# Fourier products over all 128 rows, with channel 128 and token 128 added as columns on VectorE

## The chip, the cores and the metric

The kernel runs on 1 core of one Trainium2 chip. The metric is the device time in microseconds of one execution. Three runs of the kernel before took 1964.46, 1966.94 and 1972.05 us (median 1966.94). A further execution was profiled; all rows below come from it.

## The reference, cut to what matters

Two layers of a diffusion backbone work on 256 context tokens and 256 latent tokens of width 1024. Each layer projects the normed input with `w_in`, runs three branches (mLSTM, differential attention, a Fourier mixing), merges them under sigmoid gates, projects with `w_out`, and applies a SwiGLU feed-forward. The last layer computes only the latent tokens. The Fourier branch takes the 2-D transform over the tokens and over the 256 channels of each of four groups, and keeps the real part:

```python
def _fourier(u):
    B, T, _ = u.shape
    z = u.astype(jnp.float32).reshape(B, T, FN_GROUPS, FN_GC)
    y = jnp.fft.fftn(z, axes=(1, 3), norm='ortho').real
    return y.reshape(B, T, FN_W).astype(u.dtype)

y = gm * (ym @ w_br_ml) + gd * (yd @ w_br_da) + gf * (yf @ w_br_fn)
```

## The kernel before, in words

**The main stream.** Nearly all work is a list of jobs (`prog`). A job loads 512 KB of weights (`Job.load`, L204) into one of four raw buffers, ScalarE rounds them to fp32r (`wh`, L214), VectorE takes the rest (`wl`, L224), and TensorE multiplies wh by the high part of the activations, wh by the low part, and wl by the high part (L309 to L311 in `proj_t`, L330 to L332 in `proj_n`). SP issues loads up to seven jobs ahead, splits go three jobs ahead. A job of `proj_t` has 24 products, of 512 columns in layer 0 (both segments) and 256 in layer 1 (the latent one alone).

**Side work.** A `side` is a generator that is advanced by `tick`, after each quarter of a job, at a given rate (steps divided by four times the jobs); `drain` runs what is left. The framework's planner sets the order of the instructions on each engine but SP, whose order is that of the program.

**The Fourier branch.** With the symmetry of cosine and sine, a 256-point transform splits into an even part with 129 entries and an odd part with 127. `fold_h` folds the tokens (0 to 128 and 1 to 127), `FoldZ` folds the channels of the weights, and `proj_z` computes the folded z of the four groups early in the layer. 129 does not fit in 128 rows: channel 128 of all groups comes out in rows of their own, `rn` (`last`, L837). z and rn are written to DRAM (`zscr`, `nscr`) and read back by `fourier` (L857 to L866), at job 6 of `gates(0)`.

`fourier` then runs as side `fn` beside the eight jobs of `branch(0)` (main products at L309 to L311; VectorE's L1429 evacuates each job). `ns` is the number of segments: 2 in layer 0, 1 in layer 1. Per group g of four, in fp32:

- burst 1 (`pe`): the transform over channels, even part: a full product (L890) and one with the 4 rows of rn (L891), each per segment; ScalarE copies it out (L892).
- burst 2 (`po`): the odd part (L896), and token 128 as a product with `ns` output rows (`po_x`, L899 and L900); two copies (L901, L902).
- burst 3 (`pu`): the transform over tokens: a product with the `ns` rows of token 128 (L911) and a full one (L913), once for 128 columns and once for 32 columns into `px`, and the odd part (L916); ScalarE copies `pu` out (L922), and in layer 0 VectorE subtracts for the low part (L924).

Burst 3 of a group follows the first bursts of the next one. After the last group `px` is copied out (L927, L929). `proj_fn` in `branch(2)` multiplies the result with the folded `w_br_fn` (L946 and L947 fold, L960 to L981 multiply). Side tiles of PSUM rotate over four buffers; most tiles of SBUF are 32 units of 4 KB per partition.

Of the kernel before, what the change touches and what calls it, by code (L numbers as in the profile page):

```python
# [8 lines left out]
F32 = mybir.dt.float32  # L9
# [18 lines left out]
C_ID, C_SEL, C_RC, C_RS, C_FN, C_END = 0, 128, 130, 386, 642, 1542  # L28
T_COS, T_SIN, T_C, T_S, T_ALT, T_ALT2, T_END = 0, 129, 256, 385, 513, 642, 900
VROW = {"norm1": 0, "norm2": 8, "mlhg": 16, "dahg": 24}  # L30


# [11 lines left out]
def tile_trunk(ctx: ExitStack, tc: tile.TileContext, x, c, cx, c_ctx, w_ada, b_ada, norm_g, w_in, ml_gate_b,  # L44
# [24 lines left out]
    def tmp(n=512, dt=F32):  # L69
        return tpool.tile([128, n], dt, tag="t2", name=nm("t"))  # L70
# [10 lines left out]

    cst = cpool.tile([128, C_FN], F32, tag="cst", name="cst")
    ident = cst[:, C_ID:C_ID + 128]
    sel = cst[:, C_SEL:C_SEL + 2]
    ropec = cst[:, C_RC:C_RC + 256]
    ropes = cst[:, C_RS:C_RS + 256]

# [291 lines left out]
    class AdaPart:  # L379
# [24 lines left out]
        def finish(self, scale, shift):  # L404
            pt = side_ps()
            for b in range(4):
                T.matmul(pt[:, b * 2:b * 2 + 2], lhsT=self.rows[:, b * 128:b * 128 + 128], rhs=sel, start=True, stop=True)
# [386 lines left out]
    def proj_z(l, W, ns, hf, st):  # L794

        nu, nv, w = 129 * ns, 127 * ns, 256 * ns
        per = 1024 // w
        zt = []

        def mk(g, odd):  # L800
            def run(job):
                ps = main_ps()
                if not odd and g % per == 0:
                    zt.append(unit().rearrange("p a n -> p (a n)"))

# [12 lines left out]
                if odd:  # L818
                    S.copy(o[:, nu:], ps[:, n - nv:n])
                else:  # L820
                    S.copy(o[:, :nu], ps[:, :nu])
                yield
                if odd and g == 3:
                    last()
            job = FoldZ(W[:, CZ + 256 * g + 128 * odd:CZ + 256 * g + 128 * odd + 128], KB, 128, run, ns == 2)
            job.odd, job.g, job.wn = odd, g, lambda: st["wn"]
            prog.append(job)

        def last():

            ps = side_ps()
            for k in range(KB):
                for i in range(ns):
                    T.matmul(ps[32 * (k % 4):32 * (k % 4) + 32, :nu], lhsT=st["wn"][:, k, :],
                             rhs=hf[i][k][:, :nu].bitcast(F32), start=(k < 4 and i == 0), stop=(k >= 4 and i == ns - 1))
            rn = tmp()
            S.copy(rn[:, :nu], ps[:, :nu])  # L837
# [3 lines left out]
            st["nscr"] = dpool.tile([128, 258], F32, tag="nscr", name=nm("ns"))  # L841
            nc.sync.dma_start(st["nscr"][:, :nu], rn[:, :nu])
            del zt[:]
            hf.clear()

        for g in range(4):
            mk(g, False)
            mk(g, True)
            prog[-1].mate, prog[-2].mate = prog[-2], prog[-1]

    def fourier(l, ns, st):
# [9 lines left out]
        rn = tmp()  # L861
        for g in range(4):
            nc.sync.dma_start(rn[32 * g:32 * g + 4, :nu], st["nscr"][g:128:32, :nu])
        w128 = unit().rearrange("p a n -> p (a n)")
        G.memset(w128, 0.0)
        nc.sync.dma_start(w128[31:128:32, :], w_br_fn[l, 128:1024:256, :])  # L866
        st["w128"] = [w128]
        yield
        if ns == 2:
            wh, wl = (unit(FR).rearrange("p a n -> p (a n)") for _ in range(2))  # L870
# [1 line left out]
            G.tensor_tensor(out=wl, in0=w128, in1=wh.bitcast(F32), op=ALU.subtract)  # L872
            st["w128"] = [wh, wl]
        yield
        px = side_ps()
        res = {}
        cur = None
        for g in range(5):
            prev, cur = cur, None
            if g < 4:  # L880

                z = zt[g // per][:, g % per * w:g % per * w + w]
                row = slice(32 * g, 32 * g + 4)
                ct = unit()
                xt = tmp(129)
                cur = g, ct, xt
                pe = side_ps()
                for s in range(ns):
                    c, o = slice(129 * s, 129 * s + 128), slice(129 * s, 129 * s + 129)
                    T.matmul(pe[:, o], lhsT=z[:, c], rhs=tab[:, T_C:T_C + 129], start=True, stop=False)  # L890
                    T.matmul(pe[:, o], lhsT=rn[row, c], rhs=tab[row, T_ALT:T_ALT + 129], start=False, stop=True)  # L891
                S.copy(ct[:, 0, :nu], pe[:, :nu])  # L892
                yield
                po = side_ps()
                for s in range(ns):
                    T.matmul(po[0:127, 128 * s:128 * s + 128], lhsT=z[:, nu + 127 * s:nu + 127 * s + 127],  # L896
                             rhs=tab[:, T_S:T_S + 128], start=True, stop=True)
                po_x = po[32 * g:32 * g + ns, 256:385]
                T.matmul(po_x, lhsT=z[:, 128:nu:129], rhs=tab[:, T_C:T_C + 129], start=True, stop=False)  # L899
                T.matmul(po_x, lhsT=rn[row, 128:nu:129], rhs=tab[row, T_ALT:T_ALT + 129], start=False, stop=True)  # L900
                S.copy(ct[0:127, 1, :128 * ns], po[0:127, :128 * ns])  # L901
                S.copy(xt[32 * g:32 * g + ns, :], po_x)  # L902
                yield
            if prev is not None:
                q, ct, xt = prev
                row = slice(32 * q, 32 * q + ns)

                pu = side_ps()
                for o, i in ((pu[:, :nu], 0), (px[32 * q:32 * q + 32, :nu], 97)):
                    n = 128 if i == 0 else 32  # L910
                    T.matmul(o, lhsT=xt[row, i:i + n], rhs=tab[row, T_ALT2:T_ALT2 + nu], start=True, stop=False)  # L911
                    for s in range(ns):
                        T.matmul(o[:, 129 * s:129 * s + 129], lhsT=ct[:, 0, 129 * s + i:129 * s + i + n],  # L913
                                 rhs=tab[:, T_COS:T_COS + 129], start=False, stop=(s == ns - 1))
                for s in range(ns):
                    T.matmul(pu[:, nu + 127 * s:nu + 127 * s + 127], lhsT=ct[0:127, 1, 128 * s:128 * s + 128],  # L916
                             rhs=tab[0:127, T_SIN:T_SIN + 127], start=True, stop=True)
# [13 lines left out]
        yield

# [398 lines left out]
    def plan(l, xget, fin, bd1, bd2, bdn):  # L1331
# [278 lines left out]
def make_consts():  # L1610
# [53 lines left out]
```

## Time and profile before

| what | value |
| --- | --- |
| median of three runs | 1966.94 us (1964.46 to 1972.05) |
| the profiled execution | 1967.22 us, span 1965.5 us |
| TensorE busy | 1910.6 us, 97% of the span |
| VectorE, ScalarE, POOL busy | 1193.9, 782.6 and 142.6 us |
| the chain that ended last | TensorE 79%, VectorE 10%, DMA 4%, ScalarE 4% |
| HBM read | 264.73 MB |

Busy time is the union of the instructions of an engine. A product's recorded duration overlaps with the next one's, so the pitch (start to start) is its cost in a stream. An fp32 product stands as two records.

### The profile page before, as it was taken

The page shows a single profiled execution, that of the slowest core. Times are in us where ns is not written, and L with a number is a line of the kernel's source. Part 1 is how long each engine was busy: PE and PEld are TensorE (multiplying, and loading weights), DVE is VectorE, ACT ScalarE, POOL GpSimd, SP SyncE. Part 2 cuts the span into 40 slices and gives each one's busy share as a digit, 9 for nine tenths or more (in the row PEclk, how much of TensorE's full clock was granted, in tenths as well). Part 3 has the DMA queues.
Part 4 walks back from the last instruction along what each step waited for, and adds up shares of the span by engine and source line. Part 5 has one row for each costly group of instructions (what it writes and reads, how often), then busy time and mean ns, then how long its engine had stood idle before and what let it go on. Part 6 is the DMA issues. An engine that isn't in the chain of part 4 may idle for free.

```text
span 1965.5 us, 27681 instructions
## 1 busy us (share of the span) xinstructions
PE 1910.6 (97%) x10504; PEld 1589.3 (81%) x10504; DVE 1193.9 (61%) x2592; ACT 782.6 (40%) x1466; POOL 142.6 (7%) x164
## 2 busy tenths in 40 slices
PE   6999999999999999999999999999999999989998
PEld 4778788888777778888777887877878888889996
DVE  4797688852476457654333235676995477576655
ACT  3233466632344323352222224322773354345443
POOL 0231100000001110000000000160100010000000
PEclk8999999999999999999999999999999999999999
DMA  9647522224322224434443332668313563555664
GB/s 307 188 137 225 174 68 62 66 87 123 112 75 86 65 82 122 153 92 152 140 149 95 115 97 70 220 195 281 103 54 86 178 196 119 151 182 167 185 196 129
DMA packets 339894, 269.48 MB, mean 137 GB/s; under 512 B 17233, under 2 KB 296145, under 8 KB 339762
## 3 DMA queue, kind: packets, MB, share of 16 engines
q1 hardware_dynamic: 339040, 265.09, 44.8%
q10 hardware_dynamic: 722, 2.62, 0.3%
q8 instruction: 83, 1.36, 0.3%
q14 instruction: 49, 0.40, 0.1%
HBM read 264.73 MB, written 7.11 MB: 138 GB/s over the span
## 4 chain that ended last, share of the span: by engine, by line
PE 79%; DVE 10%; DMA 4%; ACT 4%; issue 2%; POOL 0%; SPq 0%; DVEq 0%; ACTq 0%; POOLq 0%
PE m L309 13%; PE m L311 13%; PE m L310 13%; PE m L330 6%; PE m L332 6%; PE m L331 6%; DVE wl L224 2%; DMA wr<-in_w_in_dram 2%; PE p L1149 2%; PE m L564 2%; PE m L565 2%; PE m L563 2%; PE p L1113 1%; PE p L363 1%; PE m L678 1%
## 5 line engine op out<-in xcount | busy, mean ns | idle before, releaser
L224 DVE TENSOR_TENSOR wl<-wr,wh 128x1024 fp32r<-128x1024 f32 x336 | 420.6, 1255 | 415.2 <-ACT wh L214 412.5
L309 PE MATMUL m<-u,wh 128*128 128x512 f32 (+1 forms) x1752 | 616.3, 352 | 4.2 <-DVE u L1213 2.5
L214 ACT CAST wh<-wr 128x1024 fp32r<-128x1024 f32 x336 | 351.5, 1049 | 651.3 <-issue 227.3
L311 PE MATMUL m<-u,wl 128*128 128x512 f32 (+1 forms) x1752 | 602.4, 344 | 2.5 <-DVE wl L224 2.5
L310 PE MATMUL m<-u,wh 128*128 128x512 f32 (+1 forms) x1752 | 601.8, 344 | 0.0
L309 PEld LDWEIGHTS m<-u,wh 128*128 128x128 f32 x1752 | 332.4, 190 | 57.6 <-issue 8.0
L311 PEld LDWEIGHTS m<-u,wl 128*128 128x128 f32 x1752 | 332.3, 190 | 43.0 <-DVE wl L224 4.0
L310 PEld LDWEIGHTS m<-u,wh 128*128 128x128 f32 x1752 | 332.5, 190 | 39.0 <-issue 3.1
L330 PE MATMUL m<-wh,u 128*128 128x512 f32 x532 | 215.1, 404 | 0.0
L332 PE MATMUL m<-wh,u 128*128 128x512 f32 x532 | 208.0, 391 | 0.0
L331 PE MATMUL m<-wl,u 128*128 128x512 f32 x532 | 208.0, 391 | 0.0
L330 PEld LDWEIGHTS m<-wh,u 128*128 128x128 f32 x532 | 100.0, 188 | 25.7 <-issue 6.2
L332 PEld LDWEIGHTS m<-wh,u 128*128 128x128 f32 x532 | 99.9, 188 | 21.1
L331 PEld LDWEIGHTS m<-wl,u 128*128 128x128 f32 x532 | 100.1, 188 | 20.6 <-issue 1.4
L1255 ACT ACTIVATE u<-p,s 128x512 f32<-128x512 f32 (+1 forms) x96 | 59.3, 617 | 40.0 <-DVE s L1254 37.8
L563 PE MATMUL m<-wh,u 128*128 128x512 f32 x180 | 70.2, 390 | 0.0
L565 PE MATMUL m<-wh,u 128*128 128x512 f32 x180 | 70.1, 389 | 0.0
L564 PE MATMUL m<-wl,u 128*128 128x512 f32 x180 | 70.0, 389 | 0.0
L1214 POOL TENSOR_TENSOR u<-u,t 128x256 f32<-128x256 f32 x32 | 42.5, 1327 | 327.5 <-DVE u L1213 316.3
L1517 DVE SCALAR_TENSOR_TENSOR t<-t,m 128x512 f32<-128x512 f32 (+1 forms) x44 | 24.4, 554 | 62.9 <-PE m L311 62.4
L1252 DVE TENSOR_REDUCE s<-p 128x1 f32<-128x512 f32 (+1 forms) x96 | 57.1, 595 | 7.6 <-PE p L1250 7.4
L1212 DVE TENSOR_TENSOR t<-m,cst 32x256 f32<-32x256 f32 x128 | 53.8, 420 | 3.7 <-ACT u L1370 1.4
(288 smaller groups left out, 2499.7 us busy)
## 6 DMA issues: line engine op xcount, KB each, us to landing
wr<-in_w_in_dram SPq DMA_DIRECT2D x176, 512.0 KB
wr<-in_w_ffn_in_dram SPq DMA_DIRECT2D x88, 512.0 KB
u<-in_w_ada_dram SPq DMA_DIRECT2D x80, 512.0 KB
wr<-in_w_ffn_out_dram SPq DMA_DIRECT2D x44, 512.0 KB
u<-in_w_ada_dram SPq DMA_DIRECT2D x32, 256.0 KB
wr<-in_w_br_da_dram SPq DMA_DIRECT2D x16, 512.0 KB
wr<-in_w_br_ml_dram SPq DMA_DIRECT2D x16, 512.0 KB
wr<-in_w_out_dram SPq DMA_DIRECT2D x16, 512.0 KB
```

The source lines that it names most:

```text
L214: S.copy(self.hi, self.raw)
L224: V.tensor_tensor(out=self.lo, in0=raw, in1=self.hi, op=ALU.subtract)
L309: T.matmul(ps[:, n0:], lhsT=job.hi[:, k, :], rhs=ah, start=(k == 0), stop=False)
L310: T.matmul(ps[:, n0:], lhsT=job.hi[:, k, :], rhs=al, start=False, stop=False)
L311: T.matmul(ps[:, n0:], lhsT=job.lo[:, k, :], rhs=ah, start=False, stop=(k == KB - 1))
L330: T.matmul(st[tb], lhsT=ah, rhs=job.hi[:, j, :], start=(k == 0), stop=False)
L331: T.matmul(st[tb], lhsT=ah, rhs=job.lo[:, j, :], start=False, stop=False)
L332: T.matmul(st[tb], lhsT=al, rhs=job.hi[:, j, :], start=False, stop=(k == nk - 1))
L563: T.matmul(ps[tb], lhsT=ah, rhs=job.hi[:, j, :], start=(k == 0), stop=False)
L564: T.matmul(ps[tb], lhsT=ah, rhs=job.lo[:, j, :], start=False, stop=False)
L565: T.matmul(ps[tb], lhsT=al, rhs=job.hi[:, j, :], start=False, stop=(k == nk - 1))
L1255: S.activation(p[:, m, :nk], sp[:, :nk], AF.Exp, bias=nb, scale=0.125, accum_out=d[:, m:m + 1])
```

## The change

The products with few rows (rn, token 128) go. The even part keeps only its full products. What channel 128 adds to the transform over channels, and what token 128 adds to the transform over tokens, is a column times alternating signs; VectorE adds that while it copies out of PSUM (`add_alt`). The columns come from small products at the start (`pp`: moving operands of 4 columns or 1), which read `rn`, kept in SBUF, and two zeroed tiles `zr` and `za`. Output channel 128 of each group is collected in `px` (now SBUF) and multiplied once at the end (`pq`). The store and the loads of `nscr` go. Bursts 1 and 2 come in one step, and the side `fn` has 12 steps in place of 15. `sel` has four columns in place of two; the table loses 258 columns.

```diff
         zt = [unit().rearrange("p a n -> p (a n)") for _ in range(4 // per)]
         for i, u in enumerate(zt):
             nc.sync.dma_start(u, st["zscr"][:, 1024 * i:1024 * i + 1024])
-        rn = tmp()
-        for g in range(4):
-            nc.sync.dma_start(rn[32 * g:32 * g + 4, :nu], st["nscr"][g:128:32, :nu])
+        rn = st["rn"]
...
+        Z = unit()
+        G.memset(Z, 0.0)
+        zx = Z.rearrange("p a (b s c) -> p (a b) s c", b=2, s=2)
+        za, px, zr = zx[:, 0, :ns, :], zx[:, 1, :ns, :], zx[:, 2, :ns, :]
         yield
...
-        px = side_ps()
+        for s in range(ns):
+            V.tensor_scalar(out=zr[:, s, 31:128:32], in0=sel, scalar1=rn[:, 129 * s + 128:129 * s + 129], scalar2=None,
+                            op0=ALU.mult)
+        for i, u in enumerate(zt):
+            for s in range(ns):
+                S.copy(za[:, s, 31 + 32 * per * i:32 * per * (i + 1):32],
+                       u.rearrange("p (q n) -> p q n", q=per)[:, :, 129 * s + 128])
+        pp = side_ps()
+        for s in range(ns):
+            o, x, q = pp[:, 4 * s:4 * s + 4], pp[:, 4 * ns + s:4 * ns + s + 1], pp[:, 5 * ns + 4 * s:5 * ns + 4 * s + 4]
+            T.matmul(q, lhsT=rn[:, 129 * s:129 * s + 128], rhs=sel, start=True, stop=True)
+            T.matmul(o, lhsT=tab[:, T_ALT:T_ALT + 128], rhs=zr[:, s, 31:128:32], start=True, stop=False)
+            T.matmul(o, lhsT=tab[:, T_C:T_C + 128], rhs=za[:, s, 31:128:32], start=False, stop=True)
+            T.matmul(x, lhsT=zr[:, s, :], rhs=tab[:, T_ALT:T_ALT + 1], start=True, stop=False)
+            T.matmul(x, lhsT=za[:, s, :], rhs=tab[:, T_C + 128:T_C + 129], start=False, stop=True)
+        fcol = cpool.tile([128, 18], F32, tag="fcol", name=nm("fc"), bufs=1)
+        S.activation(fcol[:, :5 * ns], pp[:, :5 * ns], AF.Copy, scale=1.0 / 256)
+        V.tensor_copy(fcol[:, 5 * ns:9 * ns], pp[:, 5 * ns:9 * ns])
+        alt = tab[:, T_ALT:T_ALT + 129]
+        yield
+        def add_alt(out, ps, c):
+            for s in range(ns):
+                o = slice(129 * s, 129 * s + 129)
+                V.scalar_tensor_tensor(out=out[:, o], in0=alt, scalar=fcol[:, c(s):c(s) + 1], in1=ps[:, o],
+                                       op0=ALU.mult, op1=ALU.add)
...
-                    T.matmul(pe[:, o], lhsT=z[:, c], rhs=tab[:, T_C:T_C + 129], start=True, stop=False)
-                    T.matmul(pe[:, o], lhsT=rn[row, c], rhs=tab[row, T_ALT:T_ALT + 129], start=False, stop=True)
-                S.copy(ct[:, 0, :nu], pe[:, :nu])
-                yield
-                po = side_ps()
+                    T.matmul(pe[:, 129 * s:129 * s + 129], lhsT=z[:, 129 * s:129 * s + 128], rhs=tab[:, T_C:T_C + 129],
+                             start=True, stop=True)
...
-                po_x = po[32 * g:32 * g + ns, 256:385]
-                T.matmul(po_x, lhsT=z[:, 128:nu:129], rhs=tab[:, T_C:T_C + 129], start=True, stop=False)
-                T.matmul(po_x, lhsT=rn[row, 128:nu:129], rhs=tab[row, T_ALT:T_ALT + 129], start=False, stop=True)
+                add_alt(ct[:, 0, :], pe, lambda s: 5 * ns + 4 * s + g)
                 S.copy(ct[0:127, 1, :128 * ns], po[0:127, :128 * ns])
-                S.copy(xt[32 * g:32 * g + ns, :], po_x)
+                S.copy(px[:, :, 32 * g + 31], ct[:, 0, 128:nu:129])
                 yield
...
-                for o, i in ((pu[:, :nu], 0), (px[32 * q:32 * q + 32, :nu], 97)):
-                    n = 128 if i == 0 else 32
-                    T.matmul(o, lhsT=xt[row, i:i + n], rhs=tab[row, T_ALT2:T_ALT2 + nu], start=True, stop=False)
-                    for s in range(ns):
-                        T.matmul(o[:, 129 * s:129 * s + 129], lhsT=ct[:, 0, 129 * s + i:129 * s + i + n],
-                                 rhs=tab[:, T_COS:T_COS + 129], start=False, stop=(s == ns - 1))
+                for s in range(ns):
+                    T.matmul(pu[:, 129 * s:129 * s + 129], lhsT=ct[:, 0, 129 * s:129 * s + 128],
+                             rhs=tab[:, T_COS:T_COS + 129], start=True, stop=True)
...
-                S.copy(o[0], pu[:, :w])
-                if ns == 2:
-                    V.tensor_tensor(out=o[1], in0=pu[:, :w], in1=o[0], op=ALU.subtract)
+                if ns == 1:
+                    add_alt(o[0], pu, lambda s: 4 * s + q)
+                    S.copy(o[0][:, nu:], pu[:, nu:w])
+                else:
+                    v = tmp()
+                    S.copy(v[:, nu:], pu[:, nu:])
+                    add_alt(v, pu, lambda s: 4 * s + q)
+                    S.copy(o[0], v)
+                    V.tensor_tensor(out=o[1], in0=v, in1=o[0], op=ALU.subtract)
                 yield
+        pq = side_ps()
+        for s in range(ns):
+            T.matmul(pq[:, 129 * s:129 * s + 129], lhsT=px[:, s, :], rhs=tab[:, T_COS:T_COS + 129], start=True, stop=True)
...
-        side("fn", lambda: mix, 15, 8)
+        side("fn", lambda: mix, 12, 8)
```

## Rows read from the trace of the kernel before

**Rows 1.** The page: busy time, the chain by engine, the costliest group
```profile
PE 1910.6 (97%) x10504; PEld 1589.3 (81%) x10504; DVE 1193.9 (61%) x2592; ACT 782.6 (40%) x1466; POOL 142.6 (7%) x164
...
PE 79%; DVE 10%; DMA 4%; ACT 4%; issue 2%; POOL 0%; SPq 0%; DVEq 0%; ACTq 0%; POOLq 0%
...
L224 DVE TENSOR_TENSOR wl<-wr,wh 128x1024 fp32r<-128x1024 f32 x336 | 420.6, 1255 | 415.2 <-ACT wh L214 412.5
```
**Rows 2.** Stretches: window; length; busy PE, PEld, DVE, ACT, POOL; clock, DMA, GB/s
```profile
650.00:700.00 50.00, 50.00 (x236) 37.67 (x235) 18.63 (x15) 11.27 (x19) 6.91 (x6) 1.00 0.26 74
1650.00:1700.00 50.00, 50.00 (x372) 43.36 (x371) 25.99 (x41) 20.31 (x40) 6.26 (x9) 1.00 0.54 156
```
**Rows 3.** Timeline of VectorE (start, us, what): first and last L1429, both layers
```profile
656.68 0.69 DVE L1429 SCALAR_TENSOR_TENSOR t<-u,m 128x512 f32<-128x512 f32 x1 [3.31 <-PE m L311]
...
718.95 0.69 DVE L1429 SCALAR_TENSOR_TENSOR t<-u,m 128x512 f32<-128x512 f32 x1 [2.97 <-PE m L311]
...
1662.53 0.42 DVE L1429 SCALAR_TENSOR_TENSOR t<-u,m 128x256 f32<-128x256 f32 x1 [0.70 <-PE m L311]
...
1697.72 0.42 DVE L1429 SCALAR_TENSOR_TENSOR t<-u,m 128x256 f32<-128x256 f32 x1 [1.22 <-PE m L311]
```
**Rows 4.** Timeline of TensorE: main products 36 apart, then 30 apart
```profile
648.32 0.39 PE L309 MATMUL m<-u,wh 128*128 128x512 f32 x1
...
656.48 0.39 PE L309 MATMUL m<-u,wh 128*128 128x512 f32 x1
...
1659.09 0.28 PE L309 MATMUL m<-u,wh 128*128 128x256 f32 x1
...
1662.69 0.28 PE L309 MATMUL m<-u,wh 128*128 128x256 f32 x1
```
**Rows 5.** Timeline of TensorE: burst 1 of group 0, layer 0
```profile
657.84 0.38 PE L890 MATMUL p<-u,u 128*128 128x129 f32 x2
658.16 0.48 PE L891 MATMUL p<-u,t 4*128 4x129 f32 x2
658.57 0.49 PE L890 MATMUL p<-u,u 128*128 128x129 f32 x2
...
659.40 0.50 PE L309 MATMUL m<-u,wh 128*128 128x512 f32 x1
659.74 0.40 PE L310 MATMUL m<-u,wh 128*128 128x512 f32 x1
```
**Rows 6.** Timeline of TensorE: runs of narrow and of 129-column fp32 products
```profile
31.08 0.95 PE L407 MATMUL p<-cst,ar 128*128 128x2 f32 x8
31.89 0.47 PE L678 MATMUL m<-u,wh 128*128 128x512 f32 x1
...
1700.40 1.06 PE L960 MATMUL m<-u,u 128*128 128x129 f32 x8
1701.29 0.39 PE L961 MATMUL m<-u,u 128*128 128x129 f32 x2
```
**Rows 7.** Groups by form, VectorE: count, busy us, mean ns, idle before
```profile
L992 DVE TENSOR_TENSOR t<-m,t 128x127 f32<-128x127 f32 x8 | 2.3, 286 | 0.4 <-ACT t L989 0.4
```
**Rows 8.** Waits (who, for whom: us, times, longest): all engines, then TensorE's
```profile
DVE n L1156 <- ACT t L1155: 12.4, 8, 5.4
...
PE p L1201 <- DVE t L1301: 3.6, 7, 1.2
```
**Rows 9.** Timeline of POOL, layer 1
```profile
1649.47 0.96 POOL L865 MEMSET u<- 128x1024 f32 x1 [21.20 <-PE p L1201]
```
**Rows 10.** The chain that ended last, layer 1 (start, us, what)
```profile
1692.81 1.05 ACT wh L214
...
1696.53 5.00 DMA wr<-in_w_in_dram
```
**Rows 11.** Timeline of SP: the ninth load of weights from 1696.53 on
```profile
1721.64 0.37 SPq L204 DMA_DIRECT2D wr<-in_w_out_dram  x1
```
**Rows 12.** Timeline of TensorE: the last fold job but one, six pairs after 1700.40
```profile
1730.09 1.13 PE L960 MATMUL m<-u,u 128*128 128x129 f32 x8 [0.21 <-DVE u L946]
```

More of the change, by code (lines that the diff above doesn't have):

```diff
@@ L27 @@
 CQ, CK, CV, CO, CGATE, CDQ, CDK, CDV, CZ, CG = 0, 1024, 2048, 3072, 4096, 4112, 5136, 6160, 7184, 8208
-C_ID, C_SEL, C_RC, C_RS, C_FN, C_END = 0, 128, 130, 386, 642, 1542
-T_COS, T_SIN, T_C, T_S, T_ALT, T_ALT2, T_END = 0, 129, 256, 385, 513, 642, 900
+C_ID, C_SEL, C_RC, C_RS, C_FN, C_END = 0, 128, 132, 388, 644, 1286
+T_COS, T_SIN, T_C, T_S, T_ALT, T_END = 0, 129, 256, 385, 513, 642
 VROW = {"norm1": 0, "norm2": 8, "mlhg": 16, "dahg": 24}
@@ L83, in tile_trunk @@
     ident = cst[:, C_ID:C_ID + 128]
-    sel = cst[:, C_SEL:C_SEL + 2]
+    sel = cst[:, C_SEL:C_SEL + 4]
     ropec = cst[:, C_RC:C_RC + 256]
@@ L406, in finish @@
             for b in range(4):
-                T.matmul(pt[:, b * 2:b * 2 + 2], lhsT=self.rows[:, b * 128:b * 128 + 128], rhs=sel, start=True, stop=True)
+                T.matmul(pt[:, b * 2:b * 2 + 2], lhsT=self.rows[:, b * 128:b * 128 + 128], rhs=sel[:, 0:2], start=True, stop=True)
             pv = pt[:, 0:8].rearrange("p (a k r) -> p a k r", a=2, k=2)
@@ L835, in last @@
                              rhs=hf[i][k][:, :nu].bitcast(F32), start=(k < 4 and i == 0), stop=(k >= 4 and i == ns - 1))
-            rn = tmp()
-            S.copy(rn[:, :nu], ps[:, :nu])
+            st["rn"] = cpool.tile([128, 258], F32, tag="rn", name=nm("rn"), bufs=1)
+            S.copy(st["rn"][:, :nu], ps[:, :nu])
             st["zscr"] = dpool.tile([128, 4 * w], F32, tag="zscr", name=nm("zs"))
@@ L840, in last @@
                 nc.sync.dma_start(st["zscr"][:, 1024 * i:1024 * i + 1024], u)
-            st["nscr"] = dpool.tile([128, 258], F32, tag="nscr", name=nm("ns"))
-            nc.sync.dma_start(st["nscr"][:, :nu], rn[:, :nu])
             del zt[:]
@@ L860, in fourier @@
             nc.sync.dma_start(u, st["zscr"][:, 1024 * i:1024 * i + 1024])
-        rn = tmp()
-        for g in range(4):
-            nc.sync.dma_start(rn[32 * g:32 * g + 4, :nu], st["nscr"][g:128:32, :nu])
+        rn = st["rn"]
         w128 = unit().rearrange("p a n -> p (a n)")
@@ L882, in fourier @@
                 z = zt[g // per][:, g % per * w:g % per * w + w]
-                row = slice(32 * g, 32 * g + 4)
                 ct = unit()
-                xt = tmp(129)
-                cur = g, ct, xt
-                pe = side_ps()
+                cur = g, ct
+                pe, po = side_ps(), side_ps()
                 for s in range(ns):
-                    c, o = slice(129 * s, 129 * s + 128), slice(129 * s, 129 * s + 129)
-                    T.matmul(pe[:, o], lhsT=z[:, c], rhs=tab[:, T_C:T_C + 129], start=True, stop=False)
-                    T.matmul(pe[:, o], lhsT=rn[row, c], rhs=tab[row, T_ALT:T_ALT + 129], start=False, stop=True)
-                S.copy(ct[:, 0, :nu], pe[:, :nu])
-                yield
-                po = side_ps()
+                    T.matmul(pe[:, 129 * s:129 * s + 129], lhsT=z[:, 129 * s:129 * s + 128], rhs=tab[:, T_C:T_C + 129],
+                             start=True, stop=True)
                 for s in range(ns):
@@ L897, in fourier @@
                              rhs=tab[:, T_S:T_S + 128], start=True, stop=True)
-                po_x = po[32 * g:32 * g + ns, 256:385]
-                T.matmul(po_x, lhsT=z[:, 128:nu:129], rhs=tab[:, T_C:T_C + 129], start=True, stop=False)
-                T.matmul(po_x, lhsT=rn[row, 128:nu:129], rhs=tab[row, T_ALT:T_ALT + 129], start=False, stop=True)
+                add_alt(ct[:, 0, :], pe, lambda s: 5 * ns + 4 * s + g)
                 S.copy(ct[0:127, 1, :128 * ns], po[0:127, :128 * ns])
-                S.copy(xt[32 * g:32 * g + ns, :], po_x)
+                S.copy(px[:, :, 32 * g + 31], ct[:, 0, 128:nu:129])
                 yield
             if prev is not None:
-                q, ct, xt = prev
-                row = slice(32 * q, 32 * q + ns)
+                q, ct = prev
                 pu = side_ps()
-                for o, i in ((pu[:, :nu], 0), (px[32 * q:32 * q + 32, :nu], 97)):
-                    n = 128 if i == 0 else 32
-                    T.matmul(o, lhsT=xt[row, i:i + n], rhs=tab[row, T_ALT2:T_ALT2 + nu], start=True, stop=False)
-                    for s in range(ns):
-                        T.matmul(o[:, 129 * s:129 * s + 129], lhsT=ct[:, 0, 129 * s + i:129 * s + i + n],
-                                 rhs=tab[:, T_COS:T_COS + 129], start=False, stop=(s == ns - 1))
+                for s in range(ns):
+                    T.matmul(pu[:, 129 * s:129 * s + 129], lhsT=ct[:, 0, 129 * s:129 * s + 128],
+                             rhs=tab[:, T_COS:T_COS + 129], start=True, stop=True)
                 for s in range(ns):
@@ L921, in fourier @@
                 res[q] = o
-                S.copy(o[0], pu[:, :w])
-                if ns == 2:
-                    V.tensor_tensor(out=o[1], in0=pu[:, :w], in1=o[0], op=ALU.subtract)
+                if ns == 1:
[7 more added lines that the diff above has]
+                    V.tensor_tensor(out=o[1], in0=v, in1=o[0], op=ALU.subtract)
                 yield
+        pq = side_ps()
+        for s in range(ns):
+            T.matmul(pq[:, 129 * s:129 * s + 129], lhsT=px[:, s, :], rhs=tab[:, T_COS:T_COS + 129], start=True, stop=True)
         xs = unit(FR if ns == 2 else F32)
-        S.copy(xs[:, 0, :nu], px[:, :nu])
-        if ns == 2:
-            V.tensor_tensor(out=xs[:, 1, :nu], in0=px[:, :nu], in1=xs[:, 0, :nu], op=ALU.subtract)
+        if ns == 1:
+            add_alt(xs[:, 0, :], pq, lambda s: 4 * ns + s)
+        else:
+            v = tmp()
+            add_alt(v, pq, lambda s: 4 * ns + s)
+            S.copy(xs[:, 0, :nu], v[:, :nu])
+            V.tensor_tensor(out=xs[:, 1, :nu], in0=v[:, :nu], in1=xs[:, 0, :nu], op=ALU.subtract)
         st["yf"] = [res[g] for g in range(4)], xs
@@ L1615, in make_consts @@
     k[:, C_ID:C_ID + 128] = np.eye(128)
-    for r in range(2):
+    for r in range(4):
         k[r::32, C_SEL + r] = 1.0
@@ L1636, in make_consts @@
     t[:, T_ALT:T_ALT + 129] = alt
-    t[0::32, T_ALT2:T_ALT2 + 129] = alt / 256
-    t[1::32, T_ALT2 + 129:T_ALT2 + 258] = alt / 256
     k[:, C_FN:] = t
```

## The prediction

> **What bounds the kernel now.** I began with the busy shares and the chain that ended last [rows 1]: TensorE is busy for 97% of the span and holds 79% of the chain. The reader is to see that time is won or lost on TensorE, in program order, unless it waits. Next the table by stretches [rows 2], over the two stages in which the Fourier products lie: TensorE is busy in 50.00 of 50 us in both, at the full granted clock (1.00, the 2.4 GHz level), while VectorE is busy for 18.63 and 25.99 us and ScalarE for 11.27 and 20.31. There a TensorE product that is dropped comes back in full, and vector work is hidden as long as nothing that TensorE reads is late.
>
> How much of the two stages is Fourier work is read from two views together. VectorE's L1429 evacuates each of the eight products of `branch(0)`; from the first to the eighth it takes 718.95 - 656.68 = 62.27 us in layer 0 and 1697.72 - 1662.53 = 35.19 in layer 1 [rows 3]. Seven jobs of 24 main products lie between, and all Fourier products too. The main stream alone has a pitch of 8.16 us / 36 = 0.2267 us at 512 columns, 3.60 / 30 = 0.120 at 256 [rows 4]. So 168 main products take 38.1 and 20.2 us, and the Fourier products with their transitions cost **24.2 us in layer 0 and 15.0 in layer 1**. This is the pot from which the change can take: 39.2 us, 2% of the time.
>
> **Prices on TensorE.** An fp32 product is two records (x2). In layer 0's group 0 a full product followed by a short one takes 658.16 - 657.84 = 0.32 us; the short one (4 rows) before a full one takes 658.57 - 658.16 = 0.41 [rows 5]. Four full 128x129 products in a run take 1701.29 - 1700.40 = 0.89, 0.223 each [rows 6]. Four products with only two moving columns take 31.89 - 31.08 = 0.81, 0.20 each [rows 6]. The first main product after a burst takes 659.74 - 659.40 = 0.34 in place of 0.227, an exit of 0.11 [rows 5]; I use 0.10 in layer 1. I price a burst of n full products at 0.32 + (n - 1) x 0.223 + exit.
>
> **What stays and what is added.** Per group the old code has three bursts (products of `pe`; of `po` with `po_x`; of `pu` with `px`), and the new one two: `pe` with `po`, and `pu`.
> - Layer 0 (two segments): each burst has 4 full products, 0.32 + 3 x 0.223 + 0.11 = 1.10; eight of them, 8.8. The last product (`pq`, 2 products) 0.32 + 0.22 + 0.11 = 0.65. The new columns (`pp`) take 10 products with 1 or 4 moving columns, priced at the narrow 0.20: 2.0 + 0.11 = 2.1. Sum 11.6; saved 24.2 - 11.6 = **12.6 us**.
> - Layer 1 (one segment): each burst has 2 products, 0.32 + 0.22 + 0.10 = 0.64; eight, 5.2. `pq` 0.42; five narrow products 1.0 + 0.1. Sum 6.7; saved 15.0 - 6.7 = **8.3 us**.
>
> Bounds: at 0.32 for every product, full or narrow, the new sums are 34 x 0.32 + 9 x 0.11 + 10 x 0.32 + 0.1 = 15.2 and 17 x 0.32 + 9 x 0.10 + 5 x 0.32 + 0.1 = 8.0 (saved 9.0 and 7.0); at 0.20 for every product they are 9.9 and 5.4 (saved 14.3 and 9.6). I take the middle figures, since the runs of 128x129 products are the same form as the kept ones.
>
> A page speaks against the premise. The Trainium skill, "TensorE: Matmul & The Clock Gate", Part 3 (Packing small matmuls), says that products in different row groups run side by side, started about 4 ns apart. By that rule a 4-row product would ride beside its neighbours and dropping it would return next to nothing (the last rival). This trace shows the reverse: 0.41 us for the short product against 0.32 for the full one. That fits "TensorEngine Tiling (Array Packing)", Tiling Modes, by which a change of the tiling mode drains the engine.
>
> The Instruction Overhead section of that second page gives a product some 60 cycles at the least, so by it I estimate a narrow two-record product at 2 x 25 = 50 ns, and the sum would end 2.3 us lower than at 0.20. No row here shows a product so cheap.
>
> **VectorE and ScalarE.** Per group and segment two VectorE additions of 128x129 come in; the nearest row, a 128x127 addition with one PSUM operand, takes 286 ns [rows 7], so 18 in layer 0 and 9 in layer 1: 5.1 and 2.6 us, over some 57 and 31 us in which VectorE is idle for half. ScalarE loses its copies of these tiles and gets about as many small ones. I cost both at nothing; what hides them is the distance between a group's first and second burst, two side steps, 2 x 32/12 = 5.3 quarter-jobs: 7.3 us of main products in layer 0, 3.8 in layer 1. In front of an addition VectorE can have one 1.26 us split (L224, [rows 1]). One more thing lengthens the way out of PSUM: ScalarE and VectorE take turns on one PSUM tile (L1156 only reads what L1155 only reads, and waits for it, 12.4 us in 8 waits [rows 8]). In layer 0 the second burst's evacuation becomes copy, two additions, copy, subtraction, about 0.4 + 0.6 + 0.6 + 0.7 us one after the other; its readers, `proj_fn`, come a branch later.
>
> One place has no distance: `pp` reads `zr` and `za`, which VectorE and ScalarE fill in the same step. TensorE's nearest waits of this kind are those of L1201 for VectorE's L1301, 3.6 us in 7 [rows 8], so 0.5 us each, 1.2 at the longest. Bounds 0 to 1.2 per layer; I take 0.5, **1.0 us** in all.
>
> **DMA, SP and buffers.** Out go the store and four loads of `nscr` per layer on SP, and some 130 KB of table; SP's loads of weights wait for buffers, not for SP, so nothing is gained. `Z` takes one more of the 32 units. In layer 1 units are scarce: POOL's zeroing of `w128` waits until TensorE's L1201 at 1649.5 [rows 9]. `Z` comes behind it on POOL and gets the next unit; units come free through L1201's run, long before `pp` at about 1663. Nothing on SP waits for `Z`. Cost nothing, at worst 1 us.
>
> **What is late next.** In layer 1 the chain leaves TensorE just behind these products: from ScalarE's split at 1692.81 over VectorE and a 5.00 us load issued at 1696.53 [rows 10], and at 1730.09 TensorE waits 0.21 us for a folded weight (L946) [rows 12]. SP issues eight loads from 1696.53 to 1721.64 [rows 10, 11], 3.14 us each; TensorE consumes one per (1730.09 - 1700.40)/12 = 2.47 [rows 6, 12]. So the loader falls behind through `branch(2)` and its lead is just used up at the end. In the new `branch(0)` a job takes (35.19 - 8.3)/7 = 3.84 us, still above 3.14, so the loader arrives with nearly its old lead. What TensorE saves after 1692.81 (the last `pu`, 1.1, less `pq`, 0.4) it must wait for instead, and some of what came shortly before. I take **1.5 us**; bounds 0 and all 8.3.
>
> **Sum.** 12.6 + 8.3 - 1.0 - 1.5 = 18.4 us off the profiled execution's 1967.22 (span 1965.5 and 1.7 around it), which lies 0.3 above the median of the runs, 1966.94. Forecast **1948.8 us**, 0.94% less.
>
> **Rivals.** 0.5% (9.8 us) is what a measurement of this kernel can tell from no change, so faster means below 1957.1.
> - *The loader takes layer 1's gain.* For it: [rows 10 to 12], four raw buffers, a 5 us landing. Against it: the pace of 3.84. Then 1967.2 - 12.6 + 1.0 = 1955.6 us. Chance 0.15, of which a third lands above 1957.1.
> - *The additions are on the path.* The second burst waits for VectorE, which stands behind an L224. For it: VectorE's order is the planner's. Against it: 3.8 us of distance. At 1.2 us for each of eight groups, 9.6 us go: 1958.4 us. Chance 0.07, no change.
> - *Slower.* In layer 1 the queue of VectorE holds an addition that waits for TensorE in front of an L224 or L946; that releases the raw buffer later, and the loader's loop slows. 24 loads run from here to the end of `w_out`; 18.4 us are used up when each comes 0.77 us later, and at 1.2 us later the time is 1967.2 - 18.4 + 28.8 = 1977.6. For it: TensorE has no lead left at 1730. Against it: VectorE is idle for half of the stage. Chance 0.07.
> - *The change does not do what it says.* The short products were nearly free, and full ones get dearer without them. Then only the full-row ones count (`po_x` 0.32 and `px` 0.55 a group in layer 0, as two products with the second at 0.23, 0.32 + 0.32 in layer 1): 3.5 + 2.6 less 2.7 and 1.5 for new products leaves 1.9: 1965.3 us. The 0.41 excludes nearly all of it. Chance 0.03.
>
> Forecast 0.68. Faster: 0.68 + 0.10 = 0.78; within 0.5%: 0.05 + 0.07 + 0.03 = 0.15; slower 0.07. The range goes from all products at 0.20 and no waits, 1967.2 - 23.9 = 1943.3, to all at 0.32 with 2.4 us of waits and layer 1's gain gone, 1967.2 - 9.0 + 2.4 = 1960.6: it leaves out the slower rival and the last one.
>
> **What would show it.** L1429's first to eighth: 62.3 to about 51 us and 35.2 to about 28. No product with 1, 2 or 4 rows. TensorE's waits on `pp`'s line under 1.2 us. TensorE's idle time between 1690 and 1735 of the old count under 2 us. I am wrong if TensorE waits for a vector addition in every group, if main products in the stage slow down, or if stretches far from the Fourier stages move.

## The result and the profile after

The changed kernel takes 1945.63 us (median of four runs, 1943.74 to 1946.12) beside 1966.74 for the kernel before (four runs, 1964.46 to 1972.05): ratio 0.9885, 95% interval 0.9871 to 0.9899, 1.1% less. The forecast was 1948.8 with a range of 1943.3 to 1960.6. The profiled execution took 1945.3 us.

The page of the changed kernel, the lines that answer to [rows 1]:

```profile
span 1943.6 us, 27563 instructions
PE 1887.5 (97%) x10428; PEld 1582.6 (81%) x10428; DVE 1200.3 (62%) x2624; ACT 780.7 (40%) x1468; POOL 144.7 (7%) x166
PE 80%; DVE 10%; ACT 4%; DMA 3%; issue 2%; POOL 0%; SPq 0%; DVEq 0%; ACTq 0%; POOLq 0%
```

TensorE is busy for 23.1 us less, VectorE for 6.4 us more, and the span is 21.9 us shorter: TensorE still sets the time, and what it no longer does comes back.

VectorE's timeline, first and last evacuation of `branch(0)` in both layers (L1460 now; it answers to L1429 in [rows 3]):

```profile
656.54 0.69 DVE L1460 SCALAR_TENSOR_TENSOR t<-u,m 128x512 f32<-128x512 f32 x1 [3.31 <-PE m L311]
...
706.39 0.69 DVE L1460 SCALAR_TENSOR_TENSOR t<-u,m 128x512 f32<-128x512 f32 x1
...
1649.33 0.42 DVE L1460 SCALAR_TENSOR_TENSOR t<-u,m 128x256 f32<-128x256 f32 x1 [0.69 <-PE m L311]
...
1674.44 0.68 DVE L978 TENSOR_TENSOR u<-wr 128x512 f32<-128x512 f32 x1
1675.04 0.41 DVE L1460 SCALAR_TENSOR_TENSOR t<-u,m 128x256 f32<-128x256 f32 x1
```

By these rows the stages went from 62.27 to 49.85 us and from 35.19 to 25.71. The last row has no idle time in front of it: VectorE came to it late, behind a fold (L978). A bracket that names TensorE says that a row marks TensorE's time; a row without one doesn't. So the table below counts on TensorE itself, from the last main product ahead of the first evacuation to the one 168 main products on.

| kernel (profiled execution), us | layer 0 | between | layer 1 | rest | span | wait for a fold | clock drop in a stage |
| --- | --- | --- | --- | --- | --- | --- | --- |
| before | 62.26 | 943.69 | 35.19 | 268.10 | 1965.5 | 0.2 | none |
| after | 49.76 | 943.13 | 25.02 | 269.57 | 1943.6 | 1.0 | layer 0 |
| after, again | 49.75 | 942.29 | 25.02 | 270.35 | 1942.3 | 1.5 | layer 0 |
| e1_split | 48.21 | 941.76 | 25.02 | 269.58 | 1938.3 | 0.8 | none |
| e6_twice | 53.56 | 942.53 | 27.68 | 270.76 | 1948.2 | 2.1 | both |
| e2_short | 54.59 | 944.44 | 27.44 | 274.36 | 1956.3 | 3.8 | layer 0 |
| e3_full | 50.00 | 941.92 | 25.89 | 270.91 | 1944.6 | 3.0 | none |
| e4_noadd | 48.19 | 946.30 | 25.03 | 270.20 | 1947.3 | 1.1 | none |
| e5_near | 48.19 | 941.30 | 25.82 | 269.43 | 1939.8 | 1.0 | none |
| e7_best | 47.81 | 943.94 | 25.02 | 268.41 | 1938.6 | 0.4 | none |
| b1_norn | 57.33 | 943.05 | 32.76 | 269.27 | 1958.5 | 1.2 | none |
| b2_notok | 53.42 | 945.72 | 28.24 | 268.14 | 1949.0 | 0.3 | none |
| e8_light | 48.19 | 945.96 | 25.03 | 268.54 | 1945.2 | none | none |

Layer 0 gives 12.50 us, layer 1 10.17, the stretch between 0.56 and the start 0.14; the rest takes back 1.47: 21.9 together. Two kernels with the same work in a stage agree within 0.02 us at the same granted clock, while "between", which no experiment touches, runs from 941.3 to 946.3. So a term of 1 or 2 us is read from its stage and not from the whole time.

What the forecast did not have is in layer 0. TensorE's timeline of the changed kernel, the new columns (`pp`, L889 to L893) and the main products behind them:

```profile
659.07 0.28 PE L889 MATMUL p<-cst,rn 128*128 128x4 f32 x2
...
661.00 0.36 PE L893 MATMUL p<-u,u 128*128 128x1 f32 x2
661.22 0.48 PE L309 MATMUL m<-u,wh 128*128 128x512 f32 x1
661.53 0.39 PE L310 MATMUL m<-u,wh 128*128 128x512 f32 x1
...
662.38 0.63 PE L310 MATMUL m<-u,wh 128*128 128x512 f32 x1
662.80 0.63 PE L311 MATMUL m<-u,wl 128*128 128x512 f32 x1
...
665.37 0.44 PE L311 MATMUL m<-u,wl 128*128 128x512 f32 x1
```

The ten narrow products take 661.22 - 659.07 = 2.15 us and wait for nothing. Then the main products go from a pitch of 0.227 to (665.37 - 662.38) / 7 = 0.427. The table by stretches (columns as in [rows 2]) names the cause:

```profile
661.00:663.00 2.00, 2.00 (x10) 1.68 (x10) 0.17 (x1) 0.18 (x1) 0.00 (x0) 0.76 0.92 251
663.00:665.00 2.00, 2.00 (x7) 1.52 (x6) 0.00 (x0) 0.00 (x0) 0.00 (x0) 0.50 0.00 0
665.00:667.00 2.00, 2.00 (x14) 1.77 (x12) 1.16 (x4) 1.32 (x2) 0.39 (x1) 0.89 0.00 0
```

The granted clock falls to 0.50, the 1.2 GHz level, while TensorE is busy for all of every stretch. Eight main products at 0.427 in place of 0.227 are 1.6 us.

Bursts in the stages, layer 0 (two segments), then layer 1 (one):

```profile
670.66 0.61 PE L917 MATMUL p<-u,u 128*128 128x129 f32 x4
671.11 0.61 PE L920 MATMUL p<-u,u 128*127 128x128 f32 x4
671.47 0.47 PE L309 MATMUL m<-u,wh 128*128 128x512 f32 x1
671.78 0.39 PE L310 MATMUL m<-u,wh 128*128 128x512 f32 x1
...
1653.12 0.39 PE L917 MATMUL p<-u,u 128*128 128x129 f32 x2
1653.34 0.39 PE L920 MATMUL p<-u,u 128*127 128x128 f32 x2
1653.48 0.36 PE L309 MATMUL m<-u,wh 128*128 128x256 f32 x1
1653.68 0.28 PE L310 MATMUL m<-u,wh 128*128 128x256 f32 x1
```

Four products cost 671.47 - 670.66 = 0.81 and an exit of 0.31 - 0.227 = 0.08, two cost 0.36 and 0.08: no price for entering, none for the first product.

TensorE's only wait on this work is behind the stage, in `proj_fn` (L991, in [rows 12] L960):

```profile
1697.70 1.02 PE L991 MATMUL m<-u,u 128*128 128x129 f32 x7 [0.96 <-DVE u L977]
```

### The profile page after: what moved, and what is told of

Read it like the earlier page. It is cut to its first block, busy times and chain, and to the rows that moved or that the text cites. A ratio compares the mean times of both kernels' runs of the same rounds, so it can differ in the third digit from the quotient of the medians.

```text
span 1943.6 us, 27563 instructions
## 1 busy us (share of the span) xinstructions
PE 1887.5 (97%) x10428; PEld 1582.6 (81%) x10428; DVE 1200.3 (62%) x2624; ACT 780.7 (40%) x1468; POOL 144.7 (7%) x166
## 4 chain that ended last, share of the span: by engine, by line
PE 80%; DVE 10%; ACT 4%; DMA 3%; issue 2%; POOL 0%; SPq 0%; DVEq 0%; ACTq 0%; POOLq 0%
PE m L309 14%; PE m L311 14%; PE m L310 14%; PE m L330 6%; PE m L332 6%; PE m L331 6%; DVE wl L224 2%; PE p L1180 2%; PE p L363 2%; PE m L565 2%; PE m L563 2%; PE m L564 2%; PE p L1144 2%; PE m L678 1%; DMA wr<-in_w_in_dram 1%
## 5 line engine op out<-in xcount | busy, mean ns | idle before, releaser
L563 PE MATMUL m<-wh,u 128*128 128x512 f32 x180 | 70.2, 390 | 0.0
```

Source lines behind the costliest of these rows:

```text
L563: T.matmul(ps[tb], lhsT=ah, rhs=job.hi[:, j, :], start=(k == 0), stop=False)
```

## The experiments

The theory: TensorE's own program sets both stages; a product with few rows is dear because of what it costs its neighbours; the additions are hidden; a long run of narrow products can lower the clock; and behind layer 1 the fold loads take something back. Each experiment sets a rival against one part of it. Their expectations count from evacuation to evacuation, which for the changed kernel is 0.7 us more than the table in layer 1, and leaves 1.0 less for the rest. Edits are to the changed kernel unless it is said otherwise; each ratio is to runs of the kernel before that were made beside it.

### The run of narrow products: split it, double it

```diff
         for s in range(ns):
+            if s:
+                yield
...
-        side("fn", lambda: mix, 12, 8)
+        side("fn", lambda: mix, 13 if len(segs) == 2 else 12, 8)
```

> In layer 0 the products for the new columns come in two side steps (five narrow products, then five) in place of one burst of ten; nothing else changes. Theory A (the run of ten narrow products, 2.15 us, is what drops the granted clock to 0.50 from 662.0 to 665.4 in the changed kernel): the clock stays at 1.00 from 655 to 670, and the first-to-eighth L1460 of layer 0 goes from 49.85 us to about 48.3 (1.7 us of slow products less one more burst exit of 0.1). Rival B (the drop belongs to the stretch, not to the narrow products): a drop to 0.5 of some 3.4 us is there again, and the stage stays at 49.8 to 50.

Measured: 1941.66 us (1940.04 to 1941.74), ratio 0.9876 (0.9862 to 0.9891). No stretch of the stage is under 1.00; layer 0 takes 48.21.

```diff
-        for s in range(ns):
+        for s in [*range(ns)] * 2:
```

> The narrow products for the new columns are issued twice (20 in layer 0, 10 in layer 1), the result is the same. Theory A (a run of ten drops the clock): layer 1, where the five leave the clock at 1.00, now shows a drop to 0.5 behind its run of ten; its first-to-eighth L1460 goes from 25.71 to 25.71 + 5 x 0.22 + about 1 us (products of 256 columns at half the clock) = 27.8; layer 0 grows by 10 x 0.22 = 2.2 us and by some more for a longer drop. Rival B: layer 1 grows by 1.1 us alone, to 26.8, with no drop.

Measured: 1952.11 us (1949.06 to 1954.30), ratio 0.9930 (0.9914 to 0.9946). Layer 1's run is now ten products long, and its clock falls too (the stretches of e6_twice behind that run):

```profile
1652.00:1654.00 2.00, 2.00 (x17) 2.00 (x17) 0.56 (x2) 0.18 (x1) 0.00 (x0) 0.87 0.39 98
1654.00:1656.00 2.00, 2.00 (x12) 2.00 (x11) 0.01 (x1) 0.00 (x0) 0.00 (x0) 0.50 0.77 225
1656.00:1658.00 2.00, 2.00 (x15) 2.00 (x15) 1.49 (x3) 1.33 (x3) 0.74 (x1) 0.78 0.00 0
```

Layer 1 grows by 2.66 us: five products at 0.223 are 1.1, the clock the other 1.5. So the run of narrow products brings the drop about, but not each time. Of the seven profiles here with a run of exactly ten in layer 0, three have the drop (after, after again, e2_short) and four have none (e3_full, e4_noadd, e5_near, e8_light). e8_light has the same TensorE program there; its run goes from 660.44 on, and its stretches are:

```profile
662.00:664.00 2.00, 2.00 (x13) 1.78 (x13) 0.17 (x1) 0.18 (x1) 0.00 (x0) 1.00 0.91 259
664.00:666.00 2.00, 2.00 (x13) 1.71 (x13) 0.36 (x1) 0.55 (x1) 0.00 (x0) 1.00 0.01 4
```

Its 48.19 beside 49.76 is the price of the drop: 1.57 us. Since four profiles with the run of ten have no drop, e1_split's missing one alone would show little. What carries the reading is the count: of the 26 stages in the table, nine have ten or more narrow products in a row, and five of these have a drop; of the 17 others, with runs of five or fewer or with none, no stage has one. What decides at ten stays open.

### A product with 4 rows, and one with 128 in its place

```diff
                     T.matmul(pe[:, 129 * s:129 * s + 129], lhsT=z[:, 129 * s:129 * s + 128], rhs=tab[:, T_C:T_C + 129],
                              start=True, stop=True)
+                    T.matmul(pe[:, 258:387], lhsT=rn[32 * g:32 * g + 4, 129 * s:129 * s + 128],
+                             rhs=tab[32 * g:32 * g + 4, T_ALT:T_ALT + 129], start=True, stop=True)
```

> Behind each full product of pe a 4-row product of 129 columns is put back, into PSUM columns that nothing reads (8 in layer 0, 4 in layer 1). Theory A (a product with few rows costs more than a full one, because TensorE empties itself at each change): each brings 0.41 us of its own and makes the full one before or behind it 0.32 in place of 0.22, so 0.51 each: the stages grow from 49.85 to about 53.9 us and from 25.71 to 27.7, the whole by 6.1 us to 1951.7. Rival B (products in other row groups run beside their neighbours): under 0.05 us each, the whole unchanged at 1945.6.

Measured: 1954.80 us (1951.84 to 1957.97), ratio 0.9940 (0.9922 to 0.9958). The products go to columns of PSUM that nothing reads. TensorE's timeline of e2_short, one burst:

```profile
671.18 0.38 PE L917 MATMUL p<-u,u 128*128 128x129 f32 x2
671.49 0.48 PE L919 MATMUL p<-u,rn 4*128 4x129 f32 x2
671.91 0.49 PE L917 MATMUL p<-u,u 128*128 128x129 f32 x2
672.33 0.48 PE L919 MATMUL p<-u,rn 4*128 4x129 f32 x2
672.74 0.71 PE L922 MATMUL p<-u,u 128*127 128x128 f32 x4
673.20 0.48 PE L309 MATMUL m<-u,wh 128*128 128x512 f32 x1
```

e3_full has the same twelve products with all 128 rows (`lhsT=rn[:, ...]`, `rhs=tab[:, ...]`).

> The same 12 extra products as in the run with 4 rows, but with all 128 rows. Theory A (only the change of the row count is dear): 0.22 us each, 49.85 to about 51.6 us in layer 0, 25.71 to 26.6 in layer 1, the whole by 2.7 us to 1948.3, 3.4 us less than with 4 rows. Rival B (rows don't matter): the same time as the run with 4 rows.

Measured: 1947.99 us (1946.37 to 1951.78), ratio 0.9913 (0.9898 to 0.9928). The same burst in e3_full:

```profile
669.30 0.38 PE L917 MATMUL p<-u,u 128*128 128x129 f32 x2
669.52 0.39 PE L919 MATMUL p<-u,rn 128*128 128x129 f32 x2
669.74 0.39 PE L917 MATMUL p<-u,u 128*128 128x129 f32 x2
669.97 0.39 PE L919 MATMUL p<-u,rn 128*128 128x129 f32 x2
670.19 0.61 PE L922 MATMUL p<-u,u 128*127 128x128 f32 x4
670.55 0.48 PE L309 MATMUL m<-u,wh 128*128 128x512 f32 x1
```

In place of 0.81 us the burst takes 2.02 with two short products and 1.25 with two full ones: 0.60 each against 0.22. The stages agree: (54.59 - 49.76) / 8 and (27.44 - 25.02) / 4 are 0.60 both; (50.00 - 48.19) / 8, without the drop, and (25.89 - 25.02) / 4 are 0.23 and 0.22. The short product's own pitch holds only 0.42 of its 0.60 (671.91 - 671.49). The other 0.19 are in the full products beside it: those of this burst take 0.31, 0.42 and 0.46 us in place of 0.22, 0.22 and 0.36. What happens inside TensorE at such a change, no run shows.

The whole time of e2_short is 9.2 us above the changed kernel's, the stages only 7.3: behind them its wait for folds is 3.8 us, and the granted clock falls behind that wait too (0.50 from 1710 to 1712).

The rule weighed before the run, side by side in different row groups (the Trainium skill, "TensorE: Matmul & The Clock Gate", Part 3, Packing small matmuls), gives nothing to a short product between full ones: with 4 of 128 rows it is 2.7 times as dear as with all. The Trainium skill speaks there of products in different row groups, while a full product shares its rows with the short one beside it; so the prediction stretched the rule, and these runs do not test it where it is stated.

### The old parts one by one, taken from the kernel before

b1_norn leaves out the products with the 4 rows of `rn` (channel 128's part of the transform over channels):

```diff
-                    T.matmul(pe[:, o], lhsT=z[:, c], rhs=tab[:, T_C:T_C + 129], start=True, stop=False)
-                    T.matmul(pe[:, o], lhsT=rn[row, c], rhs=tab[row, T_ALT:T_ALT + 129], start=False, stop=True)
+                    T.matmul(pe[:, o], lhsT=z[:, c], rhs=tab[:, T_C:T_C + 129], start=True, stop=True)
```

> The kernel before with one part of the change alone: the 4-row products of pe (L891) are left out, and with them what channel 128 adds to the even part; all else stays. Theory A (a 4-row product costs 0.60 us, as the run with them put back showed): layer 0's first-to-eighth goes from 62.3 us to 57.5, layer 1's from 35.2 to 32.8, the whole by 7.2 us to about 1959.5. Rival B (0.41 us, the pitch behind it alone): 59.0 and 33.5, the whole by 4.9 us.

Measured: 1958.10 us (1956.81 to 1960.11), ratio 0.9956 (0.9940 to 0.9973). The stages lose 4.93 and 2.43 us, 0.62 and 0.61 a product.

b2_notok leaves out token 128: `po_x`, its copy into `xt`, and the products with `xt`:

```diff
-                T.matmul(po_x, lhsT=z[:, 128:nu:129], rhs=tab[:, T_C:T_C + 129], start=True, stop=False)
-                T.matmul(po_x, lhsT=rn[row, 128:nu:129], rhs=tab[row, T_ALT:T_ALT + 129], start=False, stop=True)
...
-                    T.matmul(o, lhsT=xt[row, i:i + n], rhs=tab[row, T_ALT2:T_ALT2 + nu], start=True, stop=False)
...
```

> The kernel before with the other part alone: all products for token 128 in po_x and with 1 or 2 rows (L899, L900, L911) are left out, and with them what token 128 adds; the products into px stay with their full rows. Theory A (each burst falls to the price of full products, and each that had few rows empties TensorE): layer 0's first-to-eighth goes from 62.3 us to about 53.4, layer 1's from 35.2 to 28.7, the whole by 15.4 us to about 1951. Rival B (few-row products ride beside their neighbours): less than 4 us in all.

Measured: 1949.97 us (1948.40 to 1950.76), ratio 0.9916 (0.9901 to 0.9931). The stages lose 8.84 and 6.95 us. Both parts together are 23.15; the whole change gives 22.67 in the stages. So, if the parts add up, what it adds (`pp`, `pq`, the drop) is about paid by the rest that it removes (the products into `px`, a third burst); that part was not run alone.

### The additions: leave them out, or leave them no distance

e4_noadd replaces them by one ScalarE copy (channel 128's and token 128's part is left out):

```diff
         def add_alt(out, ps, c):
-            for s in range(ns):
-                o = slice(129 * s, 129 * s + 129)
-                V.scalar_tensor_tensor(out=out[:, o], in0=alt, scalar=fcol[:, c(s):c(s) + 1], in1=ps[:, o],
-                                       op0=ALU.mult, op1=ALU.add)
+            S.copy(out[:, :nu], ps[:, :nu])
```

> The additions on VectorE (L904) are replaced by one plain ScalarE copy of the same tile; what channel 128 and token 128 add is left out of the result. Theory A (the additions are hidden by the distance between a group's two bursts): layer 1's first-to-eighth L1460 stays at 25.7 us, layer 0's at 49.85 with a drop of the clock or about 48.2 without, the whole within 1.5 us of 1945.6. Rival B (the additions are on TensorE's path): up to 1.2 us for each of eight groups comes back, the whole near 1936.

Measured: 1945.09 us (1943.53 to 1949.05), ratio 0.9899 (0.9885 to 0.9914). Layer 1 takes 25.03 beside 25.02, layer 0 48.19, as e8_light with the additions: they cost TensorE nothing.

e5_near puts a group's second burst into the step of its first one:

```diff
-        for g in range(5):
-            prev, cur = cur, None
+        for g in range(4):
...
-                yield
-            if prev is not None:
-                q, ct = prev
+                q, ct = cur
...
-        side("fn", lambda: mix, 12, 8)
+        side("fn", lambda: mix, 8, 8)
```

> The distance is taken away: a group's products over the tokens (L931, L934) come in the same step as its products over the channels (L917, L920), eight steps in place of twelve. Theory A (it is the distance that hides the additions and copies): TensorE waits in each group for the way over VectorE or ScalarE, 0.8 to 2 us eight times, less 8 saved transitions of 0.1: the whole 5 to 15 us longer than 1945.6. Rival B (the planner fills the gap with main products by itself): the waits stay under 0.3 us and the whole is at 1944 to 1946.

Measured: 1944.27 us (1941.48 to 1947.58), ratio 0.9893 (0.9878 to 0.9907). The expected waits did not come. TensorE's timeline of e5_near, group 0 in layer 0, and a group in layer 1:

```profile
668.90 0.61 PE L919 MATMUL p<-u,u 128*127 128x128 f32 x4
669.26 0.47 PE L309 MATMUL m<-u,wh 128*128 128x512 f32 x1
669.57 0.40 PE L310 MATMUL m<-u,wh 128*128 128x512 f32 x1
669.81 0.61 PE L928 MATMUL p<-u,u 128*128 128x129 f32 x4
...
1652.48 0.49 PE L928 MATMUL p<-u,u 128*128 128x129 f32 x2
1652.72 0.36 PE L310 MATMUL m<-u,wh 128*128 128x256 f32 x1
1652.92 0.45 PE L931 MATMUL p<-u,u 127*128 127x127 f32 x2
1653.13 0.36 PE L311 MATMUL m<-u,wl 128*128 128x256 f32 x1
```

The planner needs only two main products between the bursts; by then the additions are done, and layer 0 takes 48.19, as with the distance. Layer 1 pays 0.80 us, not for a wait: there a main product stands between L928 and L931 too, and each of four groups has one transition more, 0.2 us.

### Behind the stages: half of each fold load left out

```diff
-            nc.sync.dma_start(self.raw[:, 4:8, :], rev()[:, :, cols].rearrange("g r n -> r g n"))
+            if self.do_split:
+                nc.sync.dma_start(self.raw[:, 4:8, :], rev()[:, :, cols].rearrange("g r n -> r g n"))
...
+            r2 = raw[:, 4:8, :] if self.do_split else raw[:, 0:4, :]
...
```

In layer 1 the fold then adds and subtracts the first half with itself, so the folded `w_br_fn` is not the reference's.

> The changed kernel with half of the load of each fold job of layer 1 left out (256 KB in place of 512; the first half is used twice, so the result of layer 1's branch is not the reference's). Theory A (TensorE's wait for the fold L977 in branch(2), 1.0 and 1.5 us in two profiles, is the loader's): the wait goes, and the stretch from layer 1's eighth L1460 to the end falls from 268.6 to 269.3 us to about 267.7, which is what it was before (267.8). Rival B (the wait comes from the order on VectorE, not from the loads): the wait stays at 1 us or more, the stretch at 268.5 or more.

Measured: 1943.28 us (1943.09 to 1946.90), ratio 0.9887 (0.9873 to 0.9902). TensorE's waits from 1600 to 1760 have no line for the fold any more (who, for whom: us, times, longest):

```profile
PE p L502 <- DVE u L487: 4.8, 1, 4.8
PE m L309 <- ACT wh L214: 1.1, 2, 0.7
```

The rest falls to 268.54 (267.53 from the last evacuation), beside 269.57 and 270.35 for the changed kernel and 268.10 before. Up to the first L563, in the second half of `w_out`, TensorE takes 51.43 us of it before, 52.40 and 52.95 in the changed kernel, and 51.02 in e8_light: what this part grew by, 1.0 and 1.5 us, is the wait for folded weights. The other 0.5 of the 1.47 comes later. There TensorE waits 4.8 us for VectorE's L487 in every kernel, and from within that wait on the granted clock is at the 1.2 GHz level for some 3.5 us before and some 7 in the changed kernel. Variants of the changed kernel show both (3.5 in e3_full and e7_best, 7 in e1_split and e8_light), so what sets this is open. In the whole time 1 us can't be told.

### Both remedies in one, beside the changed kernel itself

e7_best splits the columns in both layers and computes those of token 128 for both segments at once:

```diff
...
+        o = pp[:, 0:4 * ns].rearrange("p (s k) -> p s k", s=ns)
+        T.matmul(o, lhsT=tab[:, T_ALT:T_ALT + 128], rhs=zr[:, :, 31:128:32], start=True, stop=False)
+        T.matmul(o, lhsT=tab[:, T_C:T_C + 128], rhs=za[:, :, 31:128:32], start=False, stop=True)
+        yield
...
+        side("fn", lambda: mix, 13, 8)
```

> Meant to beat the changed kernel, with the same result: the narrow products for the columns in two side steps, and those for both segments that share their weights in one product (8 in place of 10 in layer 0). Theory A (ten narrow products in a run can drop the clock): no drop, layer 0's first-to-eighth 48.0 us, layer 1's 25.8, the whole 2 to 3 us below the changed kernel measured beside it. Rival B (the drop is chance and not tied to the run of narrow products): the mean of the runs is within 1 us of the changed kernel's.

> The changed kernel once more, unchanged. Theory A (whether the run of ten drops the clock depends on where in time it falls, since the kernel with 12 full products added had the same run and no drop): layer 0's first-to-eighth is either 49.9 us with a drop or 48.2 without. Rival B (always a drop): 49.9. The runs should lie at 1943.7 to 1946.2, 2 to 4 us above the version with two steps.

Measured: e7_best 1941.73 us (1940.32 to 1943.16), ratio 0.9879 (0.9864 to 0.9894); the changed kernel 1943.71 (1939.78 to 1944.60), ratio 0.9884 (0.9867 to 0.9900). e7_best has no drop and the shortest layer 0, 47.81. It is clearly faster than the kernel before; that it is faster than the changed one is shown by the stage (1.9 us less than with the drop, 0.4 less than the 48.19 of the same ten products without it), not by the times, whose intervals overlap.

## Why the prediction was right, and where it was off

- **TensorE gives back what it no longer does.** Right: busy 23.1 us less, span 21.9 less. That short products are what costs is shown by e2_short, e3_full and b1_norn; the rival that they were nearly free falls.
- **The price of a burst** was the mis-sized term: 1.10 and 0.64 forecast, 0.89 and 0.44 measured, 3.3 us over sixteen bursts (its eight bursts of 0.64 are 5.1, not 5.2). The failed step is the 0.32 for the first product. In [rows 5] that product stood before a 4-row one, and its time held a part of the short one's cost; in a burst of full products the 0.223 of [rows 6] holds for the first too. `pq` was 0.4 us too dear for the same reason.
- **The new columns:** 2.1 and 1.1 forecast; 2.15 and an exit of 0.08 in layer 0, 1.1 in layer 1. Right.
- **The waits at `pp`:** 1.0 forecast, none measured.
- **The clock** was in no term: 1.57 us. The prediction had named main products that slow down as a sign that it was wrong, and this is one. It fell together with the burst price and by luck hid most of that error in layer 0.
- **The additions** at nothing: right by e4_noadd (344 ns each against the 286 taken). The reason given, a distance of 5.3 quarter-jobs, is not needed: in e5_near two main products are enough. The two rivals that rest on VectorE fall.
- **What is late next:** 1.5 us forecast, the rest grew by 1.47. Of this 1.0 is the wait for folds, as e8_light shows; 0.5 comes later, where the clock stays low longer around the wait for L487, which no term had. So that the size fits is luck, and the wait itself varies: b1_norn saves 2.43 us in layer 1 and waits 1.2, b2_notok saves 6.95 and waits 0.3. Why it varies so is open. The rival by which the loader takes all of layer 1's gain falls.

Against the forecast's 18.4, the sum of 21.9 is 3.5 more: layer 0 0.4 (bursts and `pq` 1.9, waits 0.5, less the clock's 1.57 and 0.4 of small terms), layer 1 2.4 (bursts and `pq` 1.8, waits 0.5), and 0.7 from stretches that the change doesn't touch.

## What to carry to other kernels

Price a product from a run of its own kind: the same 128x129 product took 0.32 us before a 4-row one and 0.22 among its like, and the 4-row one cost 0.60 where its own pitch showed 0.42. When TensorE is the bound, an edge row or column of a transform is cheaper as a column that VectorE adds while it copies than as a product with few rows. Break up long runs of very narrow products, and read the granted clock in short stretches behind any new one.

## What the runs showed of the hardware

- The granted clock fell to the 1.2 GHz level (0.50 in the stretch from 663 to 665) though TensorE was busy without a gap. Ten or more products with one to four moving columns in a row came before each drop in the two stages; four profiles with the same ten had none. The Trainium skill, "TensorE: Matmul & The Clock Gate", Part 1, ties the ratio to how busy TensorE has been; the busy column alone did not show the drop here, since it stood at 2.00 of 2.00 us.
- A product with 4 rows between products with 128 cost 0.60 us, one with 128 rows 0.22.
- Narrow fp32 products with one or four moving columns ran at 0.223 us from start to start behind the first (ten took 2.15), as ones with 129 columns did.
